# Forgetting attention: one instruction per bank of scores, with the query's factor in it, and two row broadcasts instead of three

## The chip, the cores and the metric

The kernel runs on one core of one Trainium2 chip. The metric is the device time of one execution, in microseconds (us). Before the change three runs gave 774.43, 774.70 and 774.96 us, with a median of 774.7.

A core has five engines that take their instructions in order, each from a queue of its own: TensorE (PE in the profile, its weight loads PEld), VectorE (DVE), ScalarE (ACT), GpSimd (POOL) and SyncE (SP), which here issues loads alone. They wait for each other through semaphores.

## What is computed

One residual block of a streaming encoder: a feed-forward, a mixer with two branches (HGRN2 and forgetting attention), a cross-attention to a memory and a second feed-forward, with 256 tokens, width 1024 and f32 throughout. The change touches only the forgetting attention, 8 heads of 128:

```python
def fox_attention(q, k, v, f_logit):
    scale = 1.0 / math.sqrt(dh)
    c = jnp.cumsum(jax.nn.log_sigmoid(f_logit.astype(jnp.float32)), axis=1).transpose(0, 2, 1)
    ...
    def block(args):
        qi, ci, blk = args
        s = jnp.einsum('bhqd,bkhd->bhqk', qi, k32) * scale
        s = s + ci[..., None] - c[:, :, None, :]
        qpos = blk * Q_BLOCK + jnp.arange(Q_BLOCK)
        s = jnp.where(kpos[None, :] <= qpos[:, None], s, -jnp.inf)
        p = jax.nn.softmax(s, axis=-1)
        return jnp.einsum('bhqk,bkhd->bqhd', p, v32)
```

The queries, keys and values are columns of one projection of the normalized input. The normalization's factor of a token (one number, r) is not applied to the input: the kernel multiplies it in after the projection. `c` is the running sum of the logarithms of the forget gates. The query's own `ci` is the same for all keys of a row.

## The kernel before

**Matmuls.** Every f32 weight tile of 128x1024 is loaded by SyncE into one of four raw buffers, cast by ScalarE to a high part (L153) and subtracted by VectorE to a low part (L155); a product is then made of three matmuls of high and low parts (L100 records them all). A raw buffer is free for the next load once its low part is made, and there are eight buffers of each part, freed by the last matmul that reads them.

**Order.** A scheduler orders the instructions by their place in the source and their priority. The kernel overrides it in places: `with after(i)` raises the priority and lets work follow the i-th recorded matmul, and `tc.issue_after` lets an instruction follow another one. The loop over v's projection, the scores, the gates and the transposes interleave that way (constants `F_S`, `F_T`, `F_O`, `L_OA`).

**Tokens.** The 256 tokens are two halves of 128 (index h). Projections of q and k come out transposed, with channels on partitions and tokens along the free dimension, so r is needed there as a row that is broadcast over partitions (`row2`). Scores have queries on partitions, so there r is one number per partition (`r2[h]`).

**The attention, step by step.**
- L1117 to L1120: projections of k_b and q_b in groups of four heads (c), two heads at a time (j). Each head's pair of partial sums is added (`added`, L225 and L227), then each head is multiplied by `row2`, q_b also by 1/sqrt(128) (L1120, 128x256).
- `kq`, L173 and L174: keys, and the second half's queries, are split into high and low parts.
- OA: the HGRN2 output of both halves is accumulated in four banks of PSUM and scaled into `G` (L1181), which frees the banks for the second half's scores.
- `forget_sums`: `c` as 8 rows of 256 is written to DRAM (`cd`).
- L1187 to L1199: GpSimd's queue reads it back: `ct` (two loads, c with tokens on partitions), `cbc` (the first 128 tokens of all heads, broadcast to all partitions) and two `cbm` (four heads, 256 tokens each, broadcast). `affine_select` then writes 1e30 where a key is later than the query (L1198), so that subtracting masks.
- `fox_scores(h)`, L1203: for each group of four heads the scores' matmuls, then per head `p = scores + c_query - c_key` out of PSUM (L1228, and L1226 for the second half's earlier keys, each 128x128), the row maximum (L1229), four exponentials with sums (ScalarE, L1231), reciprocal and product (L1232, L1233). The first half's four heads share one bank (tag tr), the second half has two heads to a bank (tag acc, `score_psum`).
- v's projection runs on TensorE meanwhile in two banks (tag mm), each evicted by ScalarE (L1275) before it can be used again. The first gates follow in the same banks and are evicted by VectorE (`zg`, L1294). `to_T` (L385) transposes `G` in two banks (tag tr), which ScalarE (`hT`, L372) and VectorE (`lT`, L373) empty head by head before the second half's transposes can start.

Of the kernel before, what the change touches and what calls it, by code (L numbers as in the profile page):

```python
# [15 lines left out]
ALU = mybir.AluOpType  # L16
AX = mybir.AxisListType

P = 128
D = 1024  # L20
T = 256
# [7 lines left out]
BIG = 1e30  # L29
# [56 lines left out]
def block_kernel(ctx: ExitStack, tc: tile.TileContext, wts, head_in, gf_in, x_in, mem_in, memT_in, cols, rows, fbias, masks, out):  # L86
    nc = tc.nc
    V, S, G, PE = nc.vector, nc.scalar, nc.gpsimd, nc.tensor
# [10 lines left out]
    def MM(*args, **kw):  # L99
        log.append(PE.matmul(*args, **kw).ins)  # L100
# [9 lines left out]
    def nm(s):  # L110
        count[0] += 1
        return f"{s}_{count[0]}"

    def m4(shape, dt=F32, n="m"):
        return mp.tile(shape, dt, tag="m4", name=nm(n))

    def s1(n=1, dt=F32, name="s"):
        return sp.tile([P, n], dt, tag=f"s{n}", name=nm(name), bufs=16)

    def acc():  # L120
        return pp.tile([P, 512], F32, tag="acc", name=nm("acc"), bufs=4)

    def mm():
        return pp.tile([P, 512], F32, tag="mm", name=nm("mm"), bufs=2)

    def trp():
        return pp.tile([P, 512], F32, tag="tr", name=nm("tr"), bufs=2)
# [36 lines left out]
    def chunk(name, c):  # L164
        return [unit(name, 4 * c + i) for i in range(4)]
# [87 lines left out]
    def bc(a, shape, dim):  # L253
        return a.unsqueeze(dim).to_broadcast(shape)
# [102 lines left out]
    def row_of(cols2, n=2):  # L357

        runs = sp.tile([P, 64], F32, tag="runs", name=nm("runs"), bufs=1)[:, : 32 * n]
        V.transpose(runs, cols2)  # L360
        rd = dp.tile([n, 4, 32], F32, name=nm("rd"))
        G.dma_start(rd.rearrange("h k t -> k h t"), runs[0:P:32].rearrange("k (h t) -> k h t", h=n))
        row = sp.tile([P, T], F32, tag="row", name=nm("row"), bufs=2)
        G.dma_start(row[:, : n * P], rd.rearrange("h k t -> (h k t)").partition_broadcast(P))
        return row
# [26 lines left out]
    def score_psum():  # L392

        return [p[:, a * T : (a + 1) * T] for p in (acc(), acc()) for a in range(2)]
# [386 lines left out]
    for kb in range(KB):  # L781
        heads.append(wp.tile([P, D], F32, tag="extra" if kb in (1, 2, 3, 4, 6) else "raw", name=nm("head"), bufs=4))
        n = HX if kb == 0 else 0
# [5 lines left out]
        if kb % 2 == 0 or kb == 1:  # L789
            a, b = ((0, 512), (512, D))[kb] if kb < 2 else (0, D)  # L790
# [32 lines left out]
    r2 = [None, None]  # L823
# [14 lines left out]
    for h in range(2):  # L838
        m = len(log)
        for c in range(2):  # L840
            ps = mm()
# [8 lines left out]
    row2 = row_of(fac[0])  # L850
# [24 lines left out]
    for c in range(2):  # L875
        u = chunk("f_a", c)
        f, k = m4([P, 2, 4, P], n="f"), m4([P, 2, 4, P], n="k")
        for j in range(2):
            fj = heads_of(f, j)
            for i in (2 * j, 2 * j + 1):  # L880
                ps = acc()
# [4 lines left out]
            for i in (2 * j, 2 * j + 1):  # L886
                hd = 4 * c + i
# [4 lines left out]
    for c in range(2):  # L892
        u = chunk("q_a", c)
        q = m4([P, 2, 4, P], n="q")
        for j in range(2):
            qj = heads_of(q, j)
            z = sp.tile([P, 2, 2, P], F32, tag="z2", name=nm("z2"), bufs=3)
            for i in range(2):
                ps = acc()
# [162 lines left out]
    for c in range(3):  # L1062
        u = [load_split(gf_in[4 * c + i], GF) for i in range(4)]
        n = min(GF, D - c * GF)
        for h in range(2):
            ps = mm()
# [11 lines left out]
    cd = dp.tile([8, T], F32, name="cd")  # L1078
# [23 lines left out]

    kb_, qb_, vb_ = [], [], []
    for c in range(2):
        for name, lst, sc in (("k_b", kb_, 1.0), ("q_b", qb_, 1.0 / math.sqrt(128.0))):
            u = chunk(name, c)
            lo_at[name, c] = los[-1]
            t = m4([P, 4, T], n=name)
            m = len(log)
            for j in range(2):  # L1110
                if c == 0 and name == "k_b":
                    ps = proj_col2(X2, u, (2 * j, 2 * j + 1))
                else:
                    for i, bank in enumerate((mm, trp)):
                        ps = bank()
                        proj_both(ps, X2, u, 2 * j + i)
                        added(t[:, 2 * j + i], ps)  # L1117
                    ps = t[:, 2 * j : 2 * j + 2]
                for i in range(2):
                    V.scalar_tensor_tensor(out=t[:, 2 * j + i], in0=ps[:, i], scalar=sc, in1=row2, op0=ALU.mult, op1=ALU.mult)  # L1120
            lst.append(t)
            if c == 0 and name == "k_b":
                forget(m + 46)
# [5 lines left out]
    for si, ms in enumerate(SETS):  # L1129
        with after(r0 + R_AT[si]):  # L1130
            banks = [acc()]
# [38 lines left out]
    for h in range(2):  # L1170
        ps = [acc(), acc()]
        for hd in range(8):
            g, i = hd // 4, hd % 4
# [10 lines left out]
        hold[_AT["v_b"] + i] = (g_last, g_last)  # L1184


    ct = s1(16, name="ct")  # L1187
    for h in range(2):
        G.dma_start(ct[:, 8 * h : 8 * h + 8], cd[:, h * P : (h + 1) * P].rearrange("e p -> p e"))
    cbc = m4([P, 8, P], n="cbc")  # L1190
    G.dma_start(cbc, cd[:, 0:P].partition_broadcast(P))
    cbm = []
    for g in range(2):
        t = m4([P, 4, T], n="cbm")
        G.dma_start(t, cd[4 * g : 4 * g + 4, :].partition_broadcast(P))
        for b, sign in ((0, 1), (1, -1)):
            tv = t[:, :, b * P : (b + 1) * P]
            G.affine_select(out=tv, in_=tv, pattern=[[0, 4], [-sign, P]], compare_op=ALU.is_ge, fill=BIG, base=0, channel_multiplier=sign)  # L1198
        cbm.append(t)  # L1199

    ps_, pT0s, pT1s = {}, [], []

    def fox_scores(h):  # L1203
        for g in range(2):
            k, q = kb_[g], qb_[g]
            ns = P * (h + 1)
            if h == 0:
                pv = trp().rearrange("p (i s) -> p i s", i=4)
                pv = [pv[:, i] for i in range(4)]
                p = sp.tile([P, 4, P], F32, tag="z2", name=nm("p0"), bufs=3)  # L1210
            else:
                pv = score_psum()
                p = m4([P, 4, T], n="p1")
            mx, sm = s1(4, name="mx"), s1(4, name="sm")
            for i in range(4):
                if h == 0:
                    MM(pv[i], q[:, i, :P], k[:, i, :ns], start=True, stop=True)
                    continue
                kp, qp = kq[g]
                for n, (a, b) in enumerate(((0, 0), (0, 1), (1, 0))):  # L1220
                    MM(pv[i], qp[:, a, i], kp[b][:, i], start=(n == 0), stop=(n == 2))
            for i in range(4):
                hd = 4 * g + i
                c1 = ct[:, h * 8 + hd : h * 8 + hd + 1]
                if h == 1:
                    V.scalar_tensor_tensor(out=p[:, i, 0:P], in0=pv[i][:, 0:P], scalar=c1, in1=cbc[:, hd], op0=ALU.add, op1=ALU.subtract)  # L1226
                ds_ = slice(h * P, (h + 1) * P)
                V.scalar_tensor_tensor(out=p[:, i, ds_], in0=pv[i][:, ds_], scalar=c1, in1=cbm[g][:, i, ds_], op0=ALU.add, op1=ALU.subtract)  # L1228
            V.tensor_reduce(out=mx, in_=p, axis=AX.X, op=ALU.max, negate=True)  # L1229
            for i in range(4):  # L1230
                S.activation(p[:, i], p[:, i], AF.Exp, bias=mx[:, i : i + 1], accum_out=sm[:, i : i + 1])  # L1231
            V.reciprocal(sm, sm)  # L1232
            V.tensor_tensor(out=p, in0=p, in1=bc(sm, [P, 4, ns], 2), op=ALU.mult)  # L1233
            ps_[g, h] = p
# [34 lines left out]
    for c in range(2):  # L1269
        u = chunk("v_b", c)  # L1270
        t = m4([P, 2, 512], n="v_b")
        for h in range(2):
            ps = mm()
# [67 lines left out]
    for c in range(2):  # L1341
        for name, X, zc in (("br_a", OA, c), ("br_b", OB, 2 + c)):
            u = chunk(name, c)
            for h in range(2):
                z = zs[zc][:, h]
                m = len(log)
                ps = mm()
# [36 lines left out]
    for c in range(2):  # L1384
        u = chunk("mk", c)
        KM.more()
        for j in range(2):
            js = slice(2 * j, 2 * j + 2)
            t = sp.tile([P, 2, T], F32, tag="z2", name=nm("km"), bufs=3)
            for i in range(2):  # L1390
                ps = acc()
# [6 lines left out]
    for c in range(2):  # L1398
        u = chunk("mq", c)
        QM.more()  # L1400
        for i in range(4):
            ps = acc()
# [3 lines left out]
            t = sp.tile([P, T], F32, tag="c1", name=nm("qm"), bufs=7)  # L1406
# [199 lines left out]
```

## Time and profile before

| | |
|---|---|
| median of three runs | 774.7 us |
| the profiled execution | 773.7 us |
| its span, first to last instruction | 771.9 us |
| TensorE clock granted, mean | 0.999 |
| HBM read | 149.25 MB |
| busy: TensorE, weight loads, VectorE, ScalarE, GpSimd | 762.5, 646.9, 639.9, 504.5, 21.6 us |

Times in the profile run from the start of the span. In a list of instructions the first column is the start, the second the duration, then engine, line, operation, output<-input and shape; xN means N of them merged, and brackets give the idle time of the engine just before and what ended it. In a list of groups, the columns behind the first bar are busy us and the mean ns of one, and behind the second the idle us before them with what ended it. Matmuls overlap, as do VectorE's records, so the time that one takes from the next is its start-to-start distance, not its duration. The attention lies between 285 and 400 us.

### The profile page before, as it was taken

The page shows a single profiled execution, that of the slowest core. Times are in us where ns is not written, and L with a number is a line of the kernel's source. Part 1 is how long each engine was busy: PE and PEld are TensorE (multiplying, and loading weights), DVE is VectorE, ACT ScalarE, POOL GpSimd, SP SyncE. Part 2 cuts the span into 40 slices and gives each one's busy share as a digit, 9 for nine tenths or more (in the row PEclk, how much of TensorE's full clock was granted, in tenths as well). Part 3 has the DMA queues.
Part 4 walks back from the last instruction along what each step waited for, and adds up shares of the span by engine and source line. Part 5 has one row for each costly group of instructions (what it writes and reads, how often), then busy time and mean ns, then how long its engine had stood idle before and what let it go on. Part 6 is the DMA issues. An engine that isn't in the chain of part 4 may idle for free.

```text
span 771.9 us, 11713 instructions
## 1 busy us (share of the span) xinstructions
PE 762.5 (99%) x4326; PEld 646.9 (84%) x4326; DVE 639.9 (83%) x967; ACT 504.5 (65%) x816; POOL 21.6 (3%) x45
## 2 busy tenths in 40 slices
PE   9999999999999999999999999999999999999996
PEld 8888788888888998898788888889888888888885
DVE  6799997997778899888776665885579899999973
ACT  8767576687775659457676444862768567675762
POOL 0000000000000101200000000000000000000000
PEclk9999999999999999999999999999999999999999
DMA  9768777674744545824567644456075716557231
GB/s 346 251 242 239 229 242 258 184 260 148 240 149 147 185 138 186 288 104 169 210 253 244 215 165 167 164 181 227 17 256 177 246 74 228 209 214 290 97 135 55
DMA packets 45338, 151.08 MB, mean 196 GB/s; under 512 B 5240, under 2 KB 8960, under 8 KB 45280
## 3 DMA queue, kind: packets, MB, share of 16 engines
q1 hardware_dynamic: 43168, 144.83, 52.8%
q0 software_dynamic: 1680, 5.13, 3.5%
q8 instruction: 34, 0.56, 0.3%
q10 hardware_dynamic: 432, 0.37, 0.1%
q14 instruction: 24, 0.20, 0.1%
HBM read 149.25 MB, written 1.06 MB: 195 GB/s over the span
## 4 chain that ended last, share of the span: by engine, by line
PE 90%; DVE 4%; ACT 2%; DMA 2%; issue 1%; DVEq 0%; ACTq 0%
PE mm L100 46%; PE acc L100 36%; PE tr L100 5%; DMA raw<-in_wts_dram 2%; PE tr L445 1%; ACT hi L153 1%; DVE lo L174 1%; PE tr L385 1%; DVE lo L155 1%; DVE sraw L592 0%; PE tr L1243 0%; DVE sx L174 0%; ACT hi L173 0%; PE tr L1337 0%; PE acc L1456 0%
## 5 line engine op out<-in xcount | busy, mean ns | idle before, releaser
L155 DVE TENSOR_TENSOR lo<-raw,hi 128x1024 fp32r<-128x1024 f32 (+1 forms) x204 | 241.3, 1199 | 34.8 <-ACT hi L153 29.8
L153 ACT CAST hi<-raw 128x1024 fp32r<-128x1024 f32 (+1 forms) x204 | 206.9, 1034 | 62.1 <-PE mm L100 28.8
L100 PE MATMUL mm<-hi,hlT 128*128 128x512 f32 (+1 forms) x688 | 209.3, 382 | 0.0
L100 PEld LDWEIGHTS mm<-hi,hlT 128*128 128x128 f32 x688 | 127.1, 188 | 22.2
L100 PE MATMUL mm<-lo,hlT 128*128 128x512 f32 (+1 forms) x344 | 130.1, 382 | 0.0
L100 PE MATMUL acc<-hi,act 128*128 128x512 f32 x352 | 114.2, 391 | 0.0
L173 ACT CAST hi<-sraw 128x1024 fp32r<-128x1024 f32 x60 | 62.5, 1053 | 23.5 <-DVE sraw L592 13.1
L100 PE MATMUL mm<-hi,sx 128*128 128x512 f32 x240 | 77.6, 389 | 0.0
L100 PEld LDWEIGHTS acc<-hi,act 128*128 128x128 f32 x352 | 66.1, 188 | 13.3
L100 PEld LDWEIGHTS mm<-lo,hlT 128*128 128x128 f32 x344 | 64.6, 188 | 10.9
L174 DVE TENSOR_TENSOR lo<-sraw,hi 128x1024 fp32r<-128x1024 f32 x60 | 72.3, 1221 | 0.9 <-ACT hi L173 0.4
L100 PE MATMUL acc<-lo,act 128*128 128x512 f32 x176 | 69.6, 396 | 0.0
L100 PE MATMUL acc<-hlT,hi 128*128 128x512 f32 x256 | 64.4, 393 | 0.0
L100 PEld LDWEIGHTS mm<-hi,sx 128*128 128x128 f32 x240 | 45.0, 188 | 9.6
L100 PEld LDWEIGHTS acc<-hlT,hi 128*128 128x128 f32 x256 | 46.1, 189 | 8.3
L100 PE MATMUL mm<-lo,sx 128*128 128x512 f32 x120 | 46.8, 390 | 0.0
L100 PEld LDWEIGHTS acc<-lo,act 128*128 128x128 f32 x176 | 33.1, 188 | 6.2
L100 PEld LDWEIGHTS acc<-hlT,lo 128*128 128x128 f32 x256 | 35.0, 190 | 2.5
L100 PE MATMUL acc<-hlT,lo 128*128 128x256 f32 x256 | 36.2, 283 | 0.0
L592 DVE TENSOR_TENSOR sraw<-sraw,raw 128x1024 f32<-128x1024 f32 x30 | 36.1, 1220 | 0.0
L174 DVE TENSOR_TENSOR lo<-raw,hi 128x1024 fp32r<-128x1024 f32 x24 | 28.8, 1219 | 0.0
L100 PEld LDWEIGHTS mm<-lo,sx 128*128 128x128 f32 x120 | 22.5, 188 | 4.7
(288 smaller groups left out, 1201.1 us busy)
## 6 DMA issues: line engine op xcount, KB each, us to landing
raw<-in_wts_dram SPq DMA_DIRECT2D x223, 512.0 KB, 4.3
sraw<-in_wts_dram SPq DMA_DIRECT2D x24, 512.0 KB, 6.3
raw<-in_gf_dram SPq DMA_DIRECT2D x12, 344.0 KB, 3.8
sraw<-in_wts_dram POOLq DMA_DIRECT2D x6, 512.0 KB, 6.6
head<-in_head_dram SPq DMA_DIRECT2D x7, 392.0 KB, 6.3
grow<-in_rows_dram SPq DMA_DIRECT2D x4, 512.0 KB, 6.4
xs<-in_x_dram SPq DMA_DIRECT2D x2, 512.0 KB, 7.4
cbm<-cd POOLq DMA_DIRECT2D x2, 512.0 KB, 5.5
```

What stands on the lines that cost most here:

```text
L100: log.append(PE.matmul(*args, **kw).ins)
L153: casts.append(S.copy(h, r).ins)
L155: los.append(V.tensor_tensor(out=l, in0=r, in1=h.bitcast(F32), op=ALU.subtract).ins)
L173: a = S.copy(hi, src)
L174: b = V.tensor_tensor(out=lo, in0=src, in1=hi.bitcast(F32), op=ALU.subtract)
L385: PE.transpose(blocks[-1][1], src(kb), ident)
L445: PE.transpose(trv[:, j, h * P : (h + 1) * P], ats[c, h][:, j * P : (j + 1) * P], ident)
L592: V.tensor_tensor(out=x, in0=x, in1=y, op=ALU.add)
```

## The change

The queries are no longer multiplied by their factor after the projection; `rq`, the factor over sqrt(128), is one number per query and goes into the eviction of the scores. The query's `ci` is left out, because a number that is the same for a whole row does not change its softmax. The eviction becomes `p = scores * rq - c_key`, one instruction for a whole bank of 512 columns. The keys are multiplied two heads at a time. `ct` and `cbc` are gone: of the two broadcasts that remain, the first 128 tokens are copied by the masking select into `cb0` for the first half, while the unmasked ones stay in place for the second half's earlier keys.

```diff
-        for name, lst, sc in (("k_b", kb_, 1.0), ("q_b", qb_, 1.0 / math.sqrt(128.0))):
+        for name, lst in (("k_b", kb_), ("q_b", qb_)):
...
-                for i in range(2):
-                    V.scalar_tensor_tensor(out=t[:, 2 * j + i], in0=ps[:, i], scalar=sc, in1=row2, op0=ALU.mult, op1=ALU.mult)
+                if name == "k_b":
+                    if len(ps.shape) == 2:
+                        ps = ps.rearrange("p (a t) -> p a t", a=2)
+                    V.tensor_tensor(out=t[:, 2 * j : 2 * j + 2], in0=ps, in1=bc(row2, [P, 2, T], 1), op=ALU.mult)
...
-    ct = s1(16, name="ct")
+    rq = []
     for h in range(2):
-        G.dma_start(ct[:, 8 * h : 8 * h + 8], cd[:, h * P : (h + 1) * P].rearrange("e p -> p e"))
-    cbc = m4([P, 8, P], n="cbc")
-    G.dma_start(cbc, cd[:, 0:P].partition_broadcast(P))
-    cbm = []
+        rq.append(s1(name="rq"))
+        V.tensor_scalar(out=rq[h], in0=r2[h], scalar1=1.0 / math.sqrt(128.0), scalar2=None, op0=ALU.mult)
+    cb = [m4([P, 8, P], n="cb0")]
     for g in range(2):
-        t = m4([P, 4, T], n="cbm")
+        t = m4([P, 4, T], n="cb1")
         G.dma_start(t, cd[4 * g : 4 * g + 4, :].partition_broadcast(P))
-        for b, sign in ((0, 1), (1, -1)):
-            tv = t[:, :, b * P : (b + 1) * P]
-            G.affine_select(out=tv, in_=tv, pattern=[[0, 4], [-sign, P]], compare_op=ALU.is_ge, fill=BIG, base=0, channel_multiplier=sign)
-        cbm.append(t)
+        for to, of_, sign in ((cb[0][:, 4 * g : 4 * g + 4], t[:, :, :P], 1), (t[:, :, P:], t[:, :, P:], -1)):
+            G.affine_select(out=to, in_=of_, pattern=[[0, 4], [-sign, P]], compare_op=ALU.is_ge, fill=BIG, base=0, channel_multiplier=sign)
+        cb.append(t)
...
-                pv = trp().rearrange("p (i s) -> p i s", i=4)
-                pv = [pv[:, i] for i in range(4)]
+                banks = [trp()]
...
-                pv = score_psum()
+                banks = [acc(), acc()]
                 p = m4([P, 4, T], n="p1")
+            pv = [b[:, a : a + ns] for b in banks for a in range(0, 512, ns)]
...
-            for i in range(4):
-                hd = 4 * g + i
-                c1 = ct[:, h * 8 + hd : h * 8 + hd + 1]
-                if h == 1:
-                    V.scalar_tensor_tensor(out=p[:, i, 0:P], in0=pv[i][:, 0:P], scalar=c1, in1=cbc[:, hd], op0=ALU.add, op1=ALU.subtract)
-                ds_ = slice(h * P, (h + 1) * P)
-                V.scalar_tensor_tensor(out=p[:, i, ds_], in0=pv[i][:, ds_], scalar=c1, in1=cbm[g][:, i, ds_], op0=ALU.add, op1=ALU.subtract)
+            n = 2 if h else 4
+            for i in range(0, 4, n):
+                c = cb[0][:, 4 * g : 4 * g + 4] if h == 0 else cb[1 + g][:, i : i + n]
+                V.scalar_tensor_tensor(out=p[:, i : i + n], in0=banks[i // n].rearrange("p (i s) -> p i s", i=n), scalar=rq[h], in1=c, op0=ALU.mult, op1=ALU.subtract)
```

The two builds list the same matmuls on TensorE and the same loads on SyncE in the same order. On VectorE the order around the change moves as the scheduler sees fit; on ScalarE, among others, the second eviction of v moves behind the first four exponentials of the second half, and the fourth behind three weight casts. On GpSimd the second broadcast follows the first one's two selects.

## The prediction

> **What bounds the kernel now.** I read the busy shares first, then the chain of waits, then the groups of TensorE with the idle time before them, and last the timelines around the attention.
>
> ```profile
> PE 762.5 (99%) x4326; PEld 646.9 (84%) x4326; DVE 639.9 (83%) x967; ACT 504.5 (65%) x816; POOL 21.6 (3%) x45
> PE 90%; DVE 4%; ACT 2%; DMA 2%; issue 1%; DVEq 0%; ACTq 0%
> ```
>
> TensorE is busy 762.5 of 771.9 us and carries 90% of the chain. Only 9.4 us of the span are without a matmul. Where these lie shows in the groups of TensorE that have idle time before them:
>
> ```profile
> L445 PE MATMUL tr<-ident,at 128*128 128x128 f32 x88 | 14.4, 274 | 0.8 <-DVE at L455 0.8
> L385 PE MATMUL tr<-ident,G 128*128 128x128 f32 x16 | 2.3, 275 | 1.1 <-DVE lT L373 1.1
> L100 PE MATMUL acc<-kp,qp 128*128 128x256 f32 x24 | 4.1, 301 | 0.1
> 766.13 0.69 DVE post L416
> ```
>
> The first is in the first feed-forward, which the diff leaves alone; the last matmul ends at about 765, and the rest is the last normalization (L416 on). What the diff can reach is the 1.1 us before the second pair of transposes of the gated HGRN2 output, and the 0.1 us before the second half's scores. In the timeline of TensorE and the chain:
>
> ```profile
> 336.95 0.38 PE L100 MATMUL tr<-k_b,q_b 128*128 128x128 f32 x2
> 337.43 0.39 PE L100 MATMUL acc<-kp,qp 128*128 128x256 f32 x1
> 373.13 0.61 PE L100 MATMUL mm<-hi,hlT 128*128 128x512 f32 x2
> 374.89 0.66 PE L385 MATMUL tr<-ident,G 128*128 128x128 f32 x4 [1.15 <-DVE lT L373]
> ...
> 342.24 18.84 PE mm L100 x83
> 361.50 5.23 DMA raw<-in_wts_dram
> 368.98 0.75 DVE zg L1294
> 374.24 0.61 DVE lT L373 x2
> ```
>
> Between these places TensorE runs back to back: 83 matmuls in 18.84 us are 0.227 us each. Two matmuls from 373.13 at that pace end at 373.58, and the next starts at 374.89: **1.30 us lost**. The two score passes from 336.95 (0.11 apart by the row) would be followed at 337.18, and 337.43 is the start: **0.25 us lost**. So 1.55 us is all that this stage can give back as long as TensorE's own work stays, and it does: both builds have the same matmuls in the same order.
>
> **The change part by part.** VectorE's groups from 285 to 356 us:
>
> ```profile
> L1120 DVE SCALAR_TENSOR_TENSOR q_b<-q_b,row 128x256 f32<-128x256 f32 x8 | 3.1, 412 | 0.1
> L1120 DVE SCALAR_TENSOR_TENSOR k_b<-k_b,row 128x256 f32<-128x256 f32 x4 | 1.8, 458 | 0.1
> L1120 DVE SCALAR_TENSOR_TENSOR k_b<-mm,row 128x256 f32<-128x256 f32 x4 | 1.5, 414 | 0.0
> L1226 DVE SCALAR_TENSOR_TENSOR p<-acc,ct,cbc 128x128 f32<-128x128 f32 x8 | 2.8, 345 | 0.0
> L1228 DVE SCALAR_TENSOR_TENSOR p<-acc,ct,cbm 128x128 f32<-128x128 f32 x8 | 2.8, 348 | 0.0
> L1228 DVE SCALAR_TENSOR_TENSOR p<-tr,ct,cbm 128x128 f32<-128x128 f32 x8 | 2.2, 344 | 0.0
> 327.75 0.75 DVE L1120 SCALAR_TENSOR_TENSOR q_b<-q_b,row 128x256 f32<-128x256 f32 x2
> 342.19 1.38 DVE L1228 SCALAR_TENSOR_TENSOR p<-tr,ct,cbm 128x128 f32<-128x128 f32 x5
> 340.40 0.74 DVE L1181 SCALAR_TENSOR_TENSOR G<-acc,rstd,G 128x512 f32<-128x512 f32 x1
> 341.06 1.22 DVE L155 TENSOR_TENSOR lo<-raw,hi 128x1024 fp32r<-128x1024 f32 x1
> 346.64 0.69 DVE L1233 TENSOR_TENSOR p<-p,sm 128x512 f32<-128x512 f32 x1
> 347.24 0.35 DVE L1226 SCALAR_TENSOR_TENSOR p<-acc,ct,cbc 128x128 f32<-128x128 f32 x1
> ```
>
> Records on VectorE overlap, so I price by start to start. Five 128x128 score steps take 1.38 us and the last record 0.34 of it: (1.38 - 0.34) / 4 = 0.26 us each. For 128x256, 0.75 - 0.41 = 0.34. One of 128x512 out of PSUM 341.06 - 340.40 = 0.66, and a 128x512 product in SBUF 347.24 - 346.64 = 0.60.
> - Scores: 24 steps of 0.26 = 6.2 us become 6 of 128x512. That form with the new mask operand is not in the trace; its bounds are 0.60 and the 0.75 of a whole record, and I take 0.66, the row with the same form and source: 4.0. Saved 2.2 (1.7 to 2.6).
> - Queries' factor: 8 x 0.34 = 2.7 us removed.
> - Keys' factor: 8 x 0.34 = 2.7 become 4 products of 0.60 to 0.66, 2.5: saved 0.2.
> - The two scaled factors (L1194 of after, 128x1) are new. I take 0.1 each and bound them by 0 and 0.25. They stand between the second reciprocal root and the step that waits for it, so most of it hides there.
>
> VectorE is rid of about 2.2 + 2.7 + 0.2 - 0.2 = 4.9 us. On the path it counts only where TensorE or something TensorE waits for stands behind it, so I follow two places.
>
> *First place.* ScalarE's cast of the second group's queries waits for the queries' factor, and four weight casts and both sums of squares stand behind it in its queue:
>
> ```profile
> 328.54 0.40 ACT L173 CAST qp<-q_b 128x256 fp32r<-128x256 f32 x1 [2.49 <-DVE q_b L1120]
> 336.62 1.41 DVE L1181 SCALAR_TENSOR_TENSOR G<-acc,rstd,G 128x512 f32<-128x512 f32 x2
> ```
>
> Without the two steps at 327.75 the cast starts 2 x 0.34 = 0.68 earlier, and so does the scaling at 336.62 that frees the score bank. That is more than 0.25, so this loss goes. What was saved before 325 us drowns: VectorE waits there for ScalarE's copies anyway, and TensorE has no idle time to give.
>
> *Second place.* Scores, weights' low parts and softmax share VectorE's queue. Each low part frees a buffer for the next weight load, whose cast ScalarE does in order ahead of the evictions hT:
>
> ```profile
> 354.50 1.21 DVE L155 TENSOR_TENSOR lo<-raw,hi 128x1024 fp32r<-128x1024 f32 x1
> 357.89 2.35 DVE L155 TENSOR_TENSOR lo<-raw,hi 128x1024 fp32r<-128x1024 f32 x2
> 360.25 1.20 DVE L155 TENSOR_TENSOR lo<-raw,hi 128x1024 fp32r<-128x1024 f32 x1
> ...
> 361.10 0.69 ACT L1275 ACTIVATE v_b<-mm,facs 128x512 f32<-128x512 f32 x1
> 362.31 1.05 ACT L153 CAST hi<-raw 128x1024 fp32r<-128x1024 f32 x1 [0.52 <-DMA raw<-in_wts_dram]
> 364.68 1.05 ACT L153 CAST hi<-raw 128x1024 fp32r<-128x1024 f32 x1 [1.31 <-DMA raw<-in_wts_dram]
> 366.76 1.05 ACT L153 CAST hi<-raw 128x1024 fp32r<-128x1024 f32 x1 [1.03 <-DMA raw<-in_wts_dram]
> 367.71 0.62 ACT L372 ACTIVATE hT<-tr,cols_s 128x128 fp32r<-128x128 f32 x2
> ...
> L1231 ACT ACTIVATE p<-p,mx 128x128 f32<-128x128 f32 (+1 forms) x16 | 7.1, 444 | 9.2 <-DVE mx L1229 9.2
> ```
>
> I laid the new order of both queues out by hand, from a scaling that ends 0.68 earlier (340.4 instead of 341.06). Prices: low part 1.13 (342.19 - 341.06), a pass over 512 columns 0.60 and over 1024 1.13, scores 0.66, a cast 0.95 and four exponentials 1.6 or 2.0 (16 in 7.1 on average). Starts, with low parts and casts counted from the first one behind v's first eviction:
>
> ```
> VectorE  low 340.4, scores 341.5, low 342.2, max 343.3, scores 343.9, max 344.6,
>          product 345.7, scores x2 346.3, scores 347.7, max 348.4, product 349.5,
>          scores 350.1, low1 350.8, max 352.1, product 353.2, low2 354.4, low3 355.5, low4 356.7
> ScalarE  exp 344.0, exp 345.6, v1 347.1, cast1-2 347.7, exp 349.6, v2 351.6, cast3-4 352.2,
>          exp 354.1, v3 356.1, cast5-7 from 356.7 as loads land, v4 near 362.6, cast8 363.3, hT 364.3
> ```
>
> Low parts 1 to 4 start at 350.8, 354.4, 355.5 and 356.7 instead of 354.5, 357.9, 359.0 and 360.25. The load behind the fourth was issued at 361.50 and cast at 366.76, 5.3 us later; 3.5 us sooner, the cast is at 363.3 and hT can start at 364.3. The next limit is the first gate's eviction zg, ahead of the low parts lT in VectorE's queue: its matmuls end at 367.0 (v's last one ends at 360.7, as the last two of the 83 above belong to the gates; 24 more are 5.45 us, and eight transposes of 0.11 stand between), 366.75 with the first place's gain. It starts near 366.9 instead of 368.98, and the seventh lT, which frees the bank, ends 2.1 sooner: 374.85 becomes 372.8. TensorE arrives at 373.3. The loss of 1.30 goes, with 0.5 us to spare.
>
> *ScalarE's order.* The second eviction of v now stands behind the first group's four exponentials, the fourth behind three weight casts. By the same layout the four end at 347.7, 352.2, 356.7 and about 363.2; TensorE asks for those banks at 349.8, 355.2, 360.7 (5.45 apart) and 367.0. Slack 2.1 us or more, so I cost this at nothing; without it each us late is a us.
>
> *GpSimd and its queue.* Gone are two small loads and one of three broadcasts of 512 KB; the second remaining broadcast now stands behind two selects.
>
> ```profile
> 311.31 0.56 POOL L1195 DMA_DIRECT2D cbm<-cd  x1 [4.80 <-PE acc L100]
> 316.75 3.03 POOL L1198 TENSOR_SCALAR_AFFINE_SELECT cbm<-cbm 128x512 f32<-128x512 f32 x4 [3.93 <-DMA cbm<-cd]
> ```
>
> At worst the second starts after two selects, 316.75 + 1.5, lands as long after its issue as the first (316.75 - 311.31 = 5.4) and has two more selects: 325.2, still 16 us ahead of the scores. Cost nothing; one load of 512 KB less may help the weights, which TensorE does not wait for here.
>
> Sum against the profiled execution: span 771.9 - 0.25 - 1.30 + about 0.1 for waits that remain but no longer last = 770.45; with the 1.8 us around the span (773.7 run) 772.25. The three runs' median is 1.0 above that run, and I carry the difference: 774.7 - 1.45 = **773.2** to the tenth, -0.19%.
>
> **The rivals.**
> *A, all of VectorE's saving passes: 769.8.* A matmul record can include waiting, so 99% busy need not mean a full TensorE: weight loads fill 84% of the span, which leaves 16%, and VectorE stands at 83%. If TensorE is fed late in many steps too small to show as idle, VectorE sets the pace of this stage and its 4.9 us pass: 774.7 - 4.9 = 769.8. Against it, 0.227 us held over 83 matmuls has no room for such steps. Chance 0.1. (By the Trainium skill, "Perfetto Trace Analysis", Identifying the Most-Contended Engine, matmul busy share is a poor measure of headroom and the share of weight loads a better one. By that rule this rival would be the likelier; the pace in the row speaks against it here.)
>
> *B, the saving is hidden: 774.5.* The wait at 374.89 hangs on loads, not on VectorE. For it: three casts in a row waited for DMA, 2.1 to 2.4 us apart, which looks like a rate. Then only 0.25 comes back. Against it: their issue followed the low parts. Chance 0.14.
>
> *C, slower: 776.3.* The fourth eviction of v, now behind three casts that wait for loads, comes after TensorE wants its bank at 367.0. With the casts at their old times (the third ends at 365.7) it would end at 366.4, just in time; it decides once the third load lands 0.6 us later than before. One load's spacing (2.2) later TensorE stops 1.6 us, and the old wait remains: 774.7 + 1.6. Against it are the earlier low parts. Chance 0.16.
>
> **How the numbers follow.** The forecast gets 0.6. About 0.2% (1.55 us) is what a measurement here can tell from no change, and 773.15 lies inside the forecast's spread of some 0.4 us, so I split it nearly evenly: faster 0.32 + 0.1 (A) = 0.42, same 0.28 + 0.14 (B) = 0.42, slower 0.16 (C). The forecast's own range, with score prices of 0.60 to 0.75 and runs that differ by 0.5, is 772.6 to 774.0. Widened to B and to the near parts of A and C: 771.8 to 775.4.
>
> **What would show it.** Right: no idle time before the transposes of G and none at 337; score steps of 0.66 start to start, six of them; the low parts in one run from about 351; hT from about 364.5. Wrong: idle time before the matmuls of the gates, with the eviction of v as releaser (C); the wait of lT still there with casts released by DMA (B); a shorter matmul pace elsewhere (A). A new wait of TensorE outside 285 to 400 us would make all of this wrong.

## The result and the profile after

The changed kernel takes **773.04 us** (median of 12 runs, 772.26 to 774.48) where the kernel before takes 774.83 on the same chip (12 runs, 774.25 to 776.18): 1.79 us less, ratio 0.9977 (95% interval 0.9968 to 0.9986). The forecast was 773.2 against 774.7. The profiled execution took 772.82 us, with a span of 771.0.

From the page of the changed kernel, busy shares and the shares of the chain:

```profile
PE 761.9 (99%) x4326; PEld 646.4 (84%) x4326; DVE 635.2 (82%) x939; ACT 505.7 (66%) x816; POOL 20.9 (3%) x42
PE 89%; DVE 5%; DMA 3%; issue 1%; ACT 1%; DVEq 0%; ACTq 0%
```

VectorE is rid of 4.7 us of busy time and of 28 instructions. TensorE bounds the kernel as before. Its groups (busy us and mean ns, then idle us and what ended them):

```profile
L445 PE MATMUL tr<-ident,at 128*128 128x128 f32 x88 | 14.4, 275 | 1.5 <-DVE at L455 1.3 <-DVE at L453 0.2
...
L100 PE MATMUL acc<-kp,qp 128*128 128x256 f32 x24 | 4.0, 298 | 0.0
...
L385 PE MATMUL tr<-ident,G 128*128 128x128 f32 x16 | 2.2, 272 | 0.0
```

The two waits that the prediction spoke of are gone. The wait in the first feed-forward, which the diff leaves alone, is longer (1.5 us, 0.8 in the profile before), and TensorE reaches the attention 0.70 us later; this is most of the reason why the two spans differ by only 0.9 us.

To measure the attention without what comes ahead of it, I cut TensorE's time there into two stages by rows that every build has: **stage 1** from the HGRN2 output's matmuls (the row of 18) to the first transposes of G, **stage 2** from there to the ninth transpose. Before:

```profile
328.60 2.17 PE L100 MATMUL acc<-iv,f 128*128 128x128 f32 x18
...
339.62 1.06 PE L100 MATMUL tr<-k_b,q_b 128*128 128x128 f32 x8
340.54 1.70 PE L100 MATMUL acc<-kp,qp 128*128 128x256 f32 x12
...
362.04 1.03 PE L385 MATMUL tr<-ident,G 128*128 128x128 f32 x8
```

and after:

```profile
329.30 2.17 PE L100 MATMUL acc<-iv,f 128*128 128x128 f32 x18
337.66 0.38 PE L100 MATMUL tr<-k_b,q_b 128*128 128x128 f32 x2
337.79 0.36 PE L100 MATMUL acc<-kp,qp 128*128 128x256 f32 x1
...
339.96 1.05 PE L100 MATMUL tr<-k_b,q_b 128*128 128x128 f32 x8
340.77 1.68 PE L100 MATMUL acc<-kp,qp 128*128 128x256 f32 x12
...
362.27 1.03 PE L385 MATMUL tr<-ident,G 128*128 128x128 f32 x8
...
373.35 0.62 PE L100 MATMUL mm<-hi,hlT 128*128 128x512 f32 x2
373.81 0.60 PE L385 MATMUL tr<-ident,G 128*128 128x128 f32 x4
```

Stage 1 goes from 33.44 to 32.97 us and stage 2 from 12.85 (374.89 - 362.04) to 11.54: 0.47 + 1.31 = 1.78 us, as much as the medians differ by. That the two agree to 0.01 us is chance: two more profiles of the kernel before, below, give 2.59 and 2.77. The 0.47 us are lost at two places. The first pass of the second half's scores starts 0.48 us behind the row ahead of it before (336.95 and 337.43 in the prediction's rows) and 0.13 after (337.66, 337.79), and the second group's first pass 0.92 (339.62, 340.54) and 0.81 (339.96, 340.77): 0.35 and 0.11 us.

TensorE's times here are 0.70 later than before (329.30 - 328.60); subtract that when setting the following rows beside the prediction. VectorE after:

```profile
337.75 1.41 DVE L1183 SCALAR_TENSOR_TENSOR G<-acc,rstd,G 128x512 f32<-128x512 f32 x2
...
340.21 0.74 DVE L1227 SCALAR_TENSOR_TENSOR p<-tr,rq,cb 128x512 f32<-128x512 f32 x1
340.87 1.22 DVE L155 TENSOR_TENSOR lo<-raw,hi 128x1024 fp32r<-128x1024 f32 x1
...
349.65 1.21 DVE L155 TENSOR_TENSOR lo<-raw,hi 128x1024 fp32r<-128x1024 f32 x1
...
353.12 2.35 DVE L155 TENSOR_TENSOR lo<-raw,hi 128x1024 fp32r<-128x1024 f32 x2
...
367.66 0.75 DVE L1293 SCALAR_TENSOR_TENSOR zg<-mm,facs,brow 128x512 f32<-128x512 f32 x1 [3.45 <-PE mm L100]
...
372.94 0.69 DVE L373 SCALAR_TENSOR_TENSOR lT<-tr,cols_s,hT 128x128 fp32r<-128x128 f32 x2
```

A whole-bank eviction takes 0.66 us to the next start (340.87 - 340.21). The first gate's eviction now waits 3.45 us for TensorE, where VectorE used to be the late one. The seventh lT is done by 373.6, just ahead of TensorE's 373.81. ScalarE after:

```profile
350.67 0.67 ACT L1274 ACTIVATE v_b<-mm,facs 128x512 f32<-128x512 f32 x1
...
355.95 0.69 ACT L1274 ACTIVATE v_b<-mm,facs 128x512 f32<-128x512 f32 x1 [0.75 <-PE mm L100]
...
358.61 1.06 ACT L153 CAST hi<-raw 128x1024 fp32r<-128x1024 f32 x1 [0.31 <-PE mm L100]
...
361.33 0.69 ACT L1274 ACTIVATE v_b<-mm,facs 128x512 f32<-128x512 f32 x1 [0.30 <-PE mm L100]
...
362.90 0.80 ACT L372 ACTIVATE hT<-tr,cols_s 128x128 fp32r<-128x128 f32 x2
```

The casts ahead of hT now wait for TensorE to free a weight buffer, no longer for loads. hT starts at 362.90, which is 5.5 us sooner than before's 367.71 once the 0.70 is subtracted.

### The profile page after: what moved, and what is told of

Same layout as the page of the kernel before. It is cut to its first block, busy times and chain, and to the rows that moved or that the text cites. A ratio compares the mean times of both kernels' runs of the same rounds, so it can differ in the third digit from the quotient of the medians.

```text
span 771.0 us, 11685 instructions
## 1 busy us (share of the span) xinstructions
PE 761.9 (99%) x4326; PEld 646.4 (84%) x4326; DVE 635.2 (82%) x939; ACT 505.7 (66%) x816; POOL 20.9 (3%) x42
## 4 chain that ended last, share of the span: by engine, by line
PE 89%; DVE 5%; DMA 3%; issue 1%; ACT 1%; DVEq 0%; ACTq 0%
PE mm L100 45%; PE acc L100 36%; PE tr L100 5%; DMA raw<-in_wts_dram 3%; DVE lo L174 1%; DVE lo L155 1%; PE tr L445 1%; PE tr L385 1%; DVE sraw L592 1%; ACT hi L173 1%; ACT hi L153 0%; PE tr L1242 0%; DVE sx L174 0%; PE tr L1336 0%; PE acc L1455 0%
## 5 line engine op out<-in xcount | busy, mean ns | idle before, releaser
L173 ACT CAST hi<-raw 128x1024 fp32r<-128x1024 f32 x24 | 24.9, 1051 | 2.4 <-issue 1.1
```

The source lines that it names most:

```text
L173: a = S.copy(hi, src)
```

## The experiments

The experiments ran on three further chips, on which the kernel before has medians of 776.5, 776.5 and 777.0 us, so ratios are compared, each to runs of the kernel before on the same chip; the 773.0 in some expectations is on the scale of the first one. The question: which of the change's parts takes away which wait, and does anything but these two waits give time? **R** is the start of the fourth scaling of G less the start of the row of 18 (the four scalings free the four score banks one after the other): 11.8 before (340.40 - 328.60), and 9.1 after (the second of the pair starts 0.67 behind 337.75). A row has one profile unless two or three values stand there; R differs by 1.0 us between the profiles of before, and by 0.01 between the two of after:

| kernel | ratio to before (95%) | stage 1 | stage 2 | R | VectorE idle ahead of zg |
|---|---|---|---|---|---|
| before | 1 | 33.44, 34.47, 34.02 | 12.85, 12.63, 13.26 | 11.8, 12.8, 12.4 | 0, 0, 0 |
| after | 0.9977 (0.9968-0.9986), 0.9975 (0.9963-0.9988) | 32.97, 32.96 | 11.54, 11.55 | 9.1, 9.1 | 3.45, 3.45 |
| bank_only | 0.9970 (0.9957-0.9983) | 32.97 | 11.55 | 11.2 | 1.76 |
| factor_only | 0.9978 (0.9964-0.9992) | 32.96 | 11.55 | 9.55 | 0.18 |
| third_load | 0.9972 (0.9957-0.9988) | 32.97 | 11.54 | 11.1 | 1.59 |
| no_max | 0.9970 (0.9955-0.9985) | 32.96 | 11.55 | 9.1 | 3.46 |
| twice | 0.9978 (0.9966-0.9990) | 32.97 | 11.77 | 9.1 | 0 |
| factor_c0 | 0.9966 (0.9952-0.9980) | 32.96 | 11.55 | 10.5 | 0.88 |
| factor_c1 | 1.0006 (0.9993-1.0018) | 32.96 | 12.91 | 11.15 | 0 |
| evict_only | 0.9981 (0.9967-0.9996) | 33.90 | 11.54 | 12.2 | 1.71 |
| two_loads | 1.0009 (0.9994-1.0024) | 32.97 | 12.19 | 11.1 | 0 |

### Both kernels once more

> The kernel before once more, for a profile beside those of the experiments, in which TensorE came 1.9 to 2.3 us later to the first quarter of the attention (from waits at 82, 118 and 171 us, which no edit touches) than in the first profile. Queue theory: the stretch from the first to the ninth transpose of G is 12.85 us again, against 11.54 in the changed kernel and in all four experiments, because the eviction of the first gate still stands 1.5 us or more behind its matmuls. Rival 'given back': where TensorE comes 2 us later it finds lT ready, the stretch is 11.5 here too, and the gain of each edit alone was read from a profile in which there was none to make.

> The kernel before a third time, for the spread of its waits from one execution to the next. Queue theory: stretch from the first to the ninth transpose of G 12.5 to 13.2 us. Rival 'given back': the later TensorE comes to the attention (first transpose of G beyond 363.5), the nearer the stretch is to 11.5.

> The changed kernel once more, beside the experiments: ratio 0.997 to 0.998; stretch between the first and the ninth transpose of G 11.54 us, VectorE idle 2 us or more before the first gate's eviction. If each part alone gives the whole gain, as the four ratios of 0.997 to 0.998 say, both together give no more than that: 2.0 us under before. If the parts add up, the two together lie 3 us or more under before.

TensorE in before_a:

```profile
331.13 2.17 PE L100 MATMUL acc<-iv,f 128*128 128x128 f32 x18
...
340.97 0.38 PE L100 MATMUL acc<-kp,qp 128*128 128x256 f32 x1 [1.10 <-DVE G L1181]
...
365.60 1.03 PE L385 MATMUL tr<-ident,G 128*128 128x128 f32 x8
...
378.23 0.66 PE L385 MATMUL tr<-ident,G 128*128 128x128 f32 x4 [0.93 <-DVE lT L373]
```

Both waits recur in all three profiles of before, also where TensorE comes 2.5 us later to the attention: the rival "given back" falls. (Stage 2 of before_b is just outside the range expected, 13.26 against 13.2.) Against the changed kernel's 44.51 us for both stages, before loses 1.78, 2.59 and 2.77 us. The second wait was typical in the first profile (1.31, then 1.09 and 1.72), the first one was not: 0.47, then 1.50 and 1.05. Stage 1 also shows where this wait begins: its length less 32.97, taken from R, leaves 11.33, 11.31 and 11.32. **At an R of 11.3 us TensorE begins to wait**, and each us beyond is a us. The rows above say the same: with nothing to wait for, TensorE asks for the second group's first bank 11.47 us behind the row of 18 (340.77 - 329.30), and where it waits, it gets it 0.14 us behind the start of the fourth scaling (340.54 - 340.40); 11.47 - 0.14 = 11.33. That bank is the third one, whose scaling starts 0.67 ahead of the fourth.

In the changed kernel the two stages repeat to 0.01 us. Its ratio shows no more gain than the parts alone do (the 3 us of a sum would be 0.996), so they don't add up.

### One part alone

bank_only: the changed kernel, with the projections as before:

```diff
-                if name == "k_b":
...
-                    V.tensor_tensor(out=t[:, 2 * j : 2 * j + 2], in0=ps, in1=bc(row2, [P, 2, T], 1), op=ALU.mult)
+                for i in range(2):
+                    V.scalar_tensor_tensor(out=t[:, 2 * j + i], in0=ps[:, i], scalar=sc, in1=row2, op0=ALU.mult, op1=ALU.mult)
...
-                V.scalar_tensor_tensor(out=p[:, i : i + n], in0=banks[i // n].rearrange("p (i s) -> p i s", i=n), scalar=rq[h], in1=c, op0=ALU.mult, op1=ALU.subtract)
+                V.tensor_tensor(out=p[:, i : i + n], in0=banks[i // n].rearrange("p (i s) -> p i s", i=n), in1=c, op=ALU.subtract)
```

> The eviction of a whole bank and the two broadcasts alone; the queries keep their factor and the keys are multiplied head by head, as before. Queue theory: the wait of the transposes of G for lT (1.30 us) is gone, because the low parts still start 2 to 3 us earlier; the wait at 337 for the scaling of G (0.2 to 0.3 us) is there again, because the queries' cast again stands behind two more steps of 0.34. Time 1.3 below the kernel before, ratio 0.998. Rival 'share': the gain is VectorE's work saved in any place, so 2.4 of the 4.9 us saved bring 2.4/4.9 of the 1.8 us measured, 0.9 us, and no single wait need come or go.

The second wait is gone, as expected, with 1.76 us to spare. The first did not come back, which was not expected: R is 11.2, a tenth under the limit. That the queries' cast stands behind two steps of 0.34 again did not decide it.

factor_only: the kernel before, with the queries' factor in the eviction:

```diff
-                for i in range(2):
-                    V.scalar_tensor_tensor(out=t[:, 2 * j + i], in0=ps[:, i], scalar=sc, in1=row2, op0=ALU.mult, op1=ALU.mult)
+                if name == "k_b":
+                    for i in range(2):
+                        V.scalar_tensor_tensor(out=t[:, 2 * j + i], in0=ps[:, i], scalar=1.0, in1=row2, op0=ALU.mult, op1=ALU.mult)
...
-                V.scalar_tensor_tensor(out=p[:, i, ds_], in0=pv[i][:, ds_], scalar=c1, in1=cbm[g][:, i, ds_], op0=ALU.add, op1=ALU.subtract)
+                V.scalar_tensor_tensor(out=p[:, i, ds_], in0=pv[i][:, ds_], scalar=rq[h], in1=cbm[g][:, i, ds_], op0=ALU.mult, op1=ALU.subtract)
```

> The kernel before, with the queries' factor alone moved into the eviction: still 24 evictions of 128x128, ct loaded but not used, three broadcasts, keys head by head. Queue theory: the wait at 337 is gone (0.25), and of the wait for lT only the 0.68 us that lie behind 325 us come off, so 0.4 to 0.7 us of idle time stay before the transposes of G; 0.9 below the kernel before. Rival 'share': 2.7/4.9 of 1.8, 1.0 us, with no wait left over at that place. The wait in the trace tells them apart, the time does not.

A miss that turned the study. I expected 0.4 to 0.7 us of the second wait to stay; none did, with 0.18 to spare, and R fell by 2.3 to 3.3 us instead of 0.68. So taking away VectorE's work **before 325 us** brings the scaling forward after all. VectorE's rows show what moves. In before_b:

```profile
309.94 0.74 DVE L1120 SCALAR_TENSOR_TENSOR q_b<-q_b,row 128x256 f32<-128x256 f32 x2
310.61 1.21 DVE L155 TENSOR_TENSOR lo<-raw,hi 128x1024 fp32r<-128x1024 f32 x1
313.88 0.42 DVE L227 TENSOR_TENSOR k_b<-mm,plo 128x256 f32<-128x256 f32 x1 [2.07 <-ACT plo L225]
314.23 1.22 DVE L155 TENSOR_TENSOR lo<-raw,hi 128x1024 fp32r<-128x1024 f32 x1
```

The copy that the add at 313.88 waited for, in ScalarE's queue:

```profile
312.53 1.05 ACT L153 CAST hi<-raw 128x1024 fp32r<-128x1024 f32 x1 [1.93 <-DMA raw<-in_wts_dram]
313.48 0.37 ACT L225 COPY plo<-mm 128x256 f32<-128x256 f32 x1
```

VectorE in factor_only:

```profile
310.17 1.20 DVE L155 TENSOR_TENSOR lo<-raw,hi 128x1024 fp32r<-128x1024 f32 x1
...
311.63 1.20 DVE L155 TENSOR_TENSOR lo<-raw,hi 128x1024 fp32r<-128x1024 f32 x1
313.09 0.42 DVE L227 TENSOR_TENSOR k_b<-mm,plo 128x256 f32<-128x256 f32 x1 [0.26 <-ACT plo L225]
```

Measured from the row of 18 (330.01 and 330.88), the first of these low parts starts 1.3 us sooner (-19.4 becomes -20.7) and the second 3.5 us sooner (-15.8 becomes -19.2); in the changed kernel they start at the same -20.7 and -19.2. Each frees a raw buffer, and the weights' loads are issued sooner: the seven behind 303 us take 15.0 us to issue in before_b and 12.6 in factor_only. With them come the casts, and the copies `plo` that stand behind the casts in ScalarE's queue. So before_b has a ring there: VectorE's add waits for a copy, the copy stands behind a cast, the cast waits for a load, and the load for a low part of VectorE. The idle time of 2.07 us that the prediction took for a cushion is a wait in this ring, and it shrinks to 0.26.

How it shrinks is not settled by that, because two more things changed with the four early steps. The second of these low parts stands behind the add in before_b and ahead of it in factor_only, so it no longer waits for the copy at all; the scheduler moved it (factor_c0, third_load and the changed kernel have that order too). And GpSimd's first broadcast is issued 2.1 us later, 20.9 us ahead of the row of 18 instead of 23.0. No run takes the steps away and keeps the order, so how much of the 3.5 us is the 1.36 us of saved work and how much the new order stays open.

### Which heads' factor?

Both are factor_only with the factor moved for one group of four heads (`scalar=rq[h] if g == 0 else 1.0` in the eviction of factor_c0; `g == 1` there and `c != 1` below in factor_c1):

```diff
-                if name == "k_b":
+                if name == "k_b" or c != 0:
```

> The kernel before, with the queries' factor moved into the eviction for the first four heads alone; their four steps on VectorE, 0.34 us each, lie between 285 and 311 us. R is the start of the fourth scaling of G less the start of the HGRN2 output's matmuls on TensorE (the row of 18): 11.8, 12.8 and 12.4 in three profiles of before, 9.1 in the changed kernel, 9.55 with the factor moved for all heads; TensorE waits at 337 where R is over 11.3. Prediction as on record ('what was saved before 325 us drowns'): R stays 11.8 to 12.8 and the wait stays. New theory (the low parts behind those steps come 1.3 to 3.5 us sooner, so the weights' loads, casts and the copies behind the casts do too): R 9.5 to 10.5, no wait at 337, and the wait for lT 0 to 0.3 instead of 1.1 to 1.7; 2.0 us under before.

> The same for the last four heads alone, whose steps lie at 321 to 333 us. Both theories: 0.68 us less on the way to the scaling. Prediction as on record: this is the whole of the factor's gain, R 9.5 to 10.5 as with all heads. New theory: R 11.1 to 12.1, only 0.7 below before; a wait of 0 to 0.8 at 337 stays, and of the wait for lT 0.4 to 1.0; 1.0 to 1.4 us under before.

VectorE ahead of zg in factor_c0, and TensorE in factor_c1:

```profile
370.03 0.75 DVE L1298 SCALAR_TENSOR_TENSOR zg<-mm,facs,brow 128x512 f32<-128x512 f32 x1 [0.88 <-PE mm L100]
```

```profile
377.12 0.66 PE L385 MATMUL tr<-ident,G 128*128 128x128 f32 x4 [1.21 <-DVE lT L373]
```

The four early steps at 285 to 311 us, which the prediction counted as drowned, take R to 10.5 and both waits away; the ratio of 0.9966 is as low as that of the whole change. The four late ones, of which it counted two, leave the second wait at 1.21, more than the 0.4 to 1.0 expected. R fell by 0.6 to 1.7 to 11.15, so the first wait goes, but the time does not follow (last part below).

### The evictions and the third broadcast

evict_only: bank_only with the two small loads and a third broadcast of 512 KB, as before:

```diff
+    ct = s1(16, name="ct")
+    for h in range(2):
+        G.dma_start(ct[:, 8 * h : 8 * h + 8], cd[:, h * P : (h + 1) * P].rearrange("e p -> p e"))
     cb = [m4([P, 8, P], n="cb0")]
+    G.dma_start(cb[0], cd[:, 0:P].partition_broadcast(P))
```

> The eviction of whole banks alone: queries' factor and keys as before, two small loads and three broadcasts of 512 KB as before. Queue theory: R 11.8 to 12.8 as before and the loss at 337 (0.5 to 1.5 us) stays, since nothing ahead of it is changed; the wait for lT is gone, because its 1.3 to 2.0 us of lateness are less than the 2.2 us that the six instructions save. 1.1 to 1.7 us under before. Rival: it gives the whole 2.0, as every part tried so far did.

two_loads: the kernel before with the first half's sums written by the select, as in the changed kernel; everything else as before:

```diff
-    cbc = m4([P, 8, P], n="cbc")
-    G.dma_start(cbc, cd[:, 0:P].partition_broadcast(P))
-    cbm = []
+    cb = [m4([P, 8, P], n="cb0")]
```

> The two broadcasts alone: 24 evictions, ct, factor and keys as before, the first half's sums copied by the select. Loads theory: R 11.2 as in the kernel with whole-bank evictions and two broadcasts, the wait at 337 gone or under 0.2, and the wait for lT shorter by the same 0.6 to 1.6 but not gone: 0 to 0.9; 1.2 to 2.0 us under before. Queue theory as on record ('cost nothing'): R 11.8 to 12.8, both waits as before, no gain.

third_load: the changed kernel with the line of evict_only that loads `cb[0]`.

> The changed kernel with a third broadcast of 512 KB in GpSimd's queue, overwritten before use, so that the traffic is that of before. Queue theory: the same time as the changed kernel within 0.3 us (773.0 where the kernel before has 774.8), no wait of TensorE for lT. Rival 'loads': what the change gave came from one transfer less beside the weights' loads; then the casts before hT wait for DMA again and 1.3 us return, 774.3.

TensorE in evict_only:

```profile
339.17 0.39 PE L100 MATMUL acc<-kp,qp 128*128 128x256 f32 x1 [0.53 <-DVE G L1181]
...
375.35 0.60 PE L385 MATMUL tr<-ident,G 128*128 128x128 f32 x4
```

The six evictions do what the prediction said, no more: the second wait is gone, the first (0.93 us of stage 1) stays, and 0.9981 is 1.5 us of 777.

The broadcast was not free, though. ScalarE in after_a, and in third_load:

```profile
318.01 2.95 ACT L153 CAST hi<-raw 128x1024 fp32r<-128x1024 f32 x3
...
322.40 1.05 ACT L153 CAST hi<-raw 128x1024 fp32r<-128x1024 f32 x1 [1.18 <-DMA raw<-in_wts_dram]
```

```profile
322.91 1.05 ACT L153 CAST hi<-raw 128x1024 fp32r<-128x1024 f32 x1 [3.30 <-DMA raw<-in_wts_dram]
...
325.69 1.05 ACT L153 CAST hi<-raw 128x1024 fp32r<-128x1024 f32 x1 [1.46 <-DMA raw<-in_wts_dram]
```

With the third broadcast the casts wait for loads 4.76 us instead of 1.18 (the three merged ones of after_a did not wait), and R rises from 9.1 to 11.1. That is under 11.3, so the time is that of the changed kernel (0.9972), as expected, but only just. In two_loads, where it alone is taken away, R falls to 11.1 and the first wait is gone; the second stays at 0.65 us. All of this was expected; the gain in time of 1.2 to 2.0 us was too, and it did not come (1.0009).

### More and less work on VectorE

no_max takes the row maximum away (`bias=ct[:, hd : hd + 1]` in the exponentials), twice issues each eviction of scores two times:

```diff
-            V.tensor_reduce(out=mx, in_=p, axis=AX.X, op=ALU.max, negate=True)
```

```diff
+                for _ in range(2):
-                V.scalar_tensor_tensor(out=p[:, i : i + n], in0=banks[i // n].rearrange("p (i s) -> p i s", i=n), scalar=rq[h], in1=c, op0=ALU.mult, op1=ALU.subtract)
+                    V.scalar_tensor_tensor(out=p[:, i : i + n], in0=banks[i // n].rearrange("p (i s) -> p i s", i=n), scalar=rq[h], in1=c, op0=ALU.mult, op1=ALU.subtract)
```

> The changed kernel without the row maximum: the exponentials take the query's ci as their bias instead, loaded by two small transfers. Softmax stays the same in exact arithmetic. VectorE is spared four more steps, about 3.5 us, between 299 and 355 us. Queue theory: TensorE has no wait left there, so nothing more is gained: 773.0 within 0.4. Rival 'share' in its strong form (VectorE sets the pace of this stage): 3.5 us more, 769.5; in its weak form (the 1.8 of 4.9 measured) 1.3 more, 771.7.

> The changed kernel with each of the six evictions of scores issued twice, to the same result: 6 x 0.66 = 4.0 us more on VectorE between 340 and 351 us. Queue theory: of the 3.45 us that VectorE stood idle ahead of the first gate's eviction all is used up, and 0.5 us passes on; TensorE loses 0 to 1 us ahead of the ninth transpose of G, time 773.3 to 774.3 where the changed kernel has 773.0. Rival 'share' (VectorE's work passes by 1.8/4.9): 1.5 us more, without a new wait at that place.

VectorE in no_max, and in twice:

```profile
359.68 1.23 DVE L155 TENSOR_TENSOR lo<-raw,hi 128x1024 fp32r<-128x1024 f32 x1 [2.21 <-ACT hi L153]
...
369.00 0.75 DVE L1296 SCALAR_TENSOR_TENSOR zg<-mm,facs,brow 128x512 f32<-128x512 f32 x1 [3.46 <-PE mm L100]
```

```profile
369.11 0.74 DVE L1294 SCALAR_TENSOR_TENSOR zg<-mm,facs,brow 128x512 f32<-128x512 f32 x1
```

Four steps less (the page has VectorE at 632.3 us of busy time, 635.2 in the changed kernel) give nothing: VectorE's idle time ahead of zg is the same 3.46 us, and what was spared comes back as waits further ahead, one of them of 2.21 us for a cast. The ratio (0.9970) excludes the 3.5 us of the rival's strong form; the 1.3 us of its weak form are excluded for this part of the kernel by the two stages, which are the same to 0.01 us. In twice, 4.0 us more (by price) use up the 3.45 us of spare time, and 0.23 us of TensorE's time comes back (stage 2: 11.77), inside the 0 to 1 us expected. The ratio cannot tell 0.23 us from nothing. Both speak against any share of VectorE's work passing by itself.

### What stays open

factor_c1 and two_loads are no faster than before (1.0006, 1.0009), although their profiles lose 1.36 and 0.65 us in the two stages against 1.78 to 2.77. By the stages factor_c1 should gain 0.4 to 1.4 us and two_loads 1.1 to 2.1. Their intervals leave room for 0.5 us at most (0.9993 and 0.9994 of 777.0), so factor_c1 may fit, and two_loads does not.

Either one profile does not stand for all executions of these builds, or they wait more elsewhere. The span less both stages is 728.9 us in factor_c1 and 729.9 in two_loads, but also 729.4 in factor_c0 and in after_a, which are faster; the three profiles of before have 725.6, 729.1 and 727.2. So factor_c1 waits no more elsewhere than factor_c0, and two_loads only 0.5 us more. This rest differs by 3.5 us between executions of one kernel, more than the whole gain, much of it by TensorE's waits in the feed-forward (0.8 to 3.2 us in the group of L445). The case of two_loads stays open.

No variant beats the changed kernel: no_max and factor_c0 (0.9970, 0.9966) have intervals that overlap with its own.

## Why the prediction was right, and where it was not

- **What bounds the stage: right.** TensorE is full but for two waits, and the attention gave back those and no more: 1.78 us by the first pair of profiles, and every build that keeps neither wait has the same two stages. Rival A is refuted by no_max: with 2.9 us less on VectorE, neither stage gets shorter. By the Trainium skill, "Perfetto Trace Analysis", Identifying the Most-Contended Engine, weight loads at 84% would leave headroom; no run here found any in these stages, since both end at the same length in every kernel that is not late.
- **The size of the first wait: too small.** The prediction put it at 0.25 us; in that same profile stage 1 loses 0.47, and in the others 1.50 and 1.05. Of the 0.47, 0.35 are at 337, where the prediction reckoned the next pass 0.10 us too late, and 0.11 at the second group's bank, which it left out. The second wait, 1.30, measured 1.31 (1.09 and 1.72 in the others). For that profile the sum of 1.45 should have been 1.78.
- **The way to the first wait: wrong step, right sign.** "What was saved before 325 us drowns: VectorE waits there for ScalarE's copies anyway" is the step that failed. Of the factor's steps the early four move R most (factor_c0), not the two at 327. R came 2.7 us sooner in the first pair of profiles where 0.68 was forecast. Had the loss been 1.50 us, as in before_a, the forecast's 0.68 would not have removed it. What the runs show in its place is that the four early steps alone bring R 1.3 to 2.3 us forward; by what share of saved work and of new order is open.
- **The second wait: right.** hT early and zg released by TensorE: it went as laid out, only faster, though the low parts came as 1, 2 and 1 and not in one run. Less the 0.70 us, hT started at 362.2 where 364.3 was laid out, and zg at 366.96 where 366.9 was. The reserve of lT was 0.2 us (373.63 against 373.81) instead of 0.5. New is how little it takes: zg was late by 1.55, 1.33 and 1.97 us in three profiles (its start behind the first transposes, 6.94 in the first, less the 5.39 of the changed kernel), and the evictions alone or the early factor alone cover that.
- **Prices: right in sum.** The eviction is 0.66, and VectorE's busy time fell by 4.7 where 4.9 was forecast from starts. The parts fit less well: 1.8 in factor_only where 2.5 was forecast (2.7 less the two new factors), 2.4 in evict_only where 2.2 was; the three profiles of before differ by 0.7.
- **ScalarE's order (rival C): right to cost it at nothing.** The third and fourth evictions of v waited for TensorE by 0.75 and 0.30 us, not TensorE for them.
- **GpSimd's queue: "cost nothing" held for the time, not for the mechanism.** "One load less may help the weights, which TensorE does not wait for here" missed that the scaling waits for them: one broadcast more puts R up by 2.0 (third_load).
- **Rival B** (loads keep the second wait) had a true core, as the casts did wait for loads; but these loads followed VectorE's low parts, and the wait went.

That the number came out within 0.2 us owes something to luck. In the profile that the forecast was built on, the first wait was the smallest of three, 0.47 us, so the 0.68 that was forecast for the scaling sufficed whatever else moved it. With the 1.05 or 1.50 of the others the same reasoning would have left a part of the wait, which the changed kernel does not have.

## What to carry to other kernels

Where engines wait in a ring (VectorE for a copy, the copy for a cast, the cast for a load, the load for a buffer that VectorE frees), idle time on one of them need not be a cushion: here, four steps of 0.34 us taken away ahead of it moved what stands behind it by 1.3 to 2.3 us. Ask what frees the buffer whose load ends the wait, and compare the order in the queues of both builds before you credit the saved time.

A saving on an engine off the critical path is worth the lateness that it removes, and no more: find how late the waiting step is, and expect several unrelated edits to give the same gain, each alone and not in sum. In this case a stage cut between two rows that every build has resolves 0.01 us where whole runs scatter by 2.

## What the chip showed unexpectedly

Weight loads of 512 KB take longer to land with one broadcast of 512 KB more beside them. DMA issues between 312 and 317.5 us (count, KB each, median us to landing), in after_a, where one broadcast is issued there, and in third_load, where two are:

```profile
raw<-in_wts_dram SPq DMA_DIRECT2D x4, 512.0 KB, 4.8
```

```profile
raw<-in_wts_dram SPq DMA_DIRECT2D x3, 512.0 KB, 8.7
```

How much longer depends on what else is under way. From 19.0 to 13.5 us ahead of the row of 18, profiles with three weight loads have medians of 4.5, 5.0, 5.5 and 5.6 us beside one broadcast (both of the changed kernel, no_max, twice) and of 7.0, 7.4 and 8.7 beside two (factor_only, factor_c0, third_load). With two weight loads it is 3.3 and 3.8 beside one (two_loads, bank_only) and 4.2 to 5.0 beside two (before three times, factor_c1, evict_only).

VectorE's steps are longer where GpSimd runs a select at the same time. Two equal products of the changed kernel, the second beside the select (VectorE, then GpSimd):

```profile
314.34 0.69 DVE L1122 TENSOR_TENSOR k_b<-k_b,row 128x512 f32<-128x512 f32 x1
...
321.58 1.11 DVE L1122 TENSOR_TENSOR k_b<-k_b,row 128x512 f32<-128x512 f32 x1
```

```profile
319.94 2.21 POOL L1200 TENSOR_SCALAR_AFFINE_SELECT cb<-cb 128x512 f32<-128x512 f32 x2 [4.97 <-DMA cb<-cd]
```

A low part of before_b is 1.65 us long beside a select, where others take 1.2. Such rows show the coincidence; that the select is the cause was not tested.
